# The second pass of the attention scores over 64 rows of the array, two heads side by side in two PSUM banks

## The chip, the cores and the metric

The kernel runs on one core of a Trainium2 chip. The metric is the device time of one execution in microseconds (us), as the median of several executions. The profile that is read below is that of one further execution of the same program.

## What is computed

A two-layer backbone over 512 latent tokens and 256 context tokens, 1024 wide. Each layer projects its input into three head groups (a short convolution, windowed attention with a sink, a gated linear attention over chunks), joins them in an output projection, and adds a gated feed-forward part. The change touches the attention scores alone, of which the reference says:

```python
ATT_HEADS, ATT_KV_HEADS, HEAD_DIM, BLOCK, WINDOW = 8, 2, 64, 128, 128
# latent queries, one block of 128 at a time, against the context keys and three blocks of latent keys
s_ctx = jnp.einsum('bqhgd,bkhd->bhgqk', qi, k_ctx).astype(jnp.float32)
s_loc = jnp.einsum('bqhgd,bkhd->bhgqk', qi, ks).astype(jnp.float32)
s_loc = jnp.where(valid, s_loc, -jnp.inf)
p = softmax_with_sink(jnp.concatenate([s_ctx, s_loc], axis=-1) * scale, sink).astype(v.dtype)
# context queries (first layer only) against the context keys
s = jnp.einsum('bqhgd,bkhd->bhgqk', qg, k).astype(jnp.float32) * HEAD_DIM ** -0.5
```

## The kernel before

**Products in parts.** TensorE multiplies in fp32r, which keeps fewer bits than fp32. So an operand is split into a high part (rounded to fp32r) and a low part (what is left, as fp32r), and a product is the sum of several passes. The dense products of the projections and of the feed-forward part take three passes (`dense_pass`: high by high, high by low, low by high) and write the PSUM tiles named `main`; everything else writes tiles named `bank`, of which there are five.

**The scores.** A head has 64 channels, half of the 128 rows of the array. The kernel uses the other half for the second part of the queries: in the tile `Q` of one query group, the 64 rows that are head `kv`'s own (0 to 63 for `kv` 0, 64 to 127 for `kv` 1) hold the high part of the queries and the other 64 rows the low part. `Kp[0]` holds the high part of the keys in both halves, `Kp[1]` the low part in both halves. The first pass, `Q` by `Kp[0]` over 128 rows, is high by high plus low by high in one matmul; the second, `Q` by `Kp[1]` over 128 rows, adds high by low plus low by low.

**One task of attention** (`attn_task`) is one block of 128 queries of one query group, both heads `kv`. A block of latent queries (four of them, in both layers, times four groups: 32 tasks) has 256 context keys, whose scores stand for both heads in the bank `pc` (256 columns each), and 256 (first and last block) or 384 (the two between) latent keys, whose scores stand in one bank for each head, `pl[0]` and `pl[1]`. Masks of the window are added by matmuls too (`identb` by `trib`, bf16, 128 columns, one for each outer block of a head). A block of context queries (two, in the first layer alone, times four: 8 tasks) has the 256 context keys alone. After the scores VectorE takes the maxima (`mx`, `mx2`), ScalarE the exponentials, and the probabilities are scaled, transposed by TensorE and multiplied with the values.

**What sets the order.** The dense passes are the main stream. A planner (class `Plan`) keeps an estimated clock of each engine, and after each step of the dense stream (`poll`) lets those tasks go on whose input should be there; up to three attention tasks are open at once. The estimate for a matmul (`mm`) goes by its columns, and for outputs of 128 partitions it does not depend on the rows that are contracted. The instructions that are recorded so are then ordered once more for each engine by the framework's scheduler, which may pull instructions of another stream between two of a task. Each engine then works through its queue in that order.

Beside the attention tasks run the tasks of the gated linear attention (`gla_task`), whose matmuls `gram` contract 64 rows into 64 partitions (64x64 quarters of the array), the products that write 64 partitions (128x64 halves), and those of the conditioning, which write 32 (128x32 quarters).

Of the kernel before, what the change touches and what calls it, by code (L numbers as in the profile page):

```python
# [13 lines left out]
AF = mybir.ActivationFunctionType  # L14
ALU = mybir.AluOpType
AX = mybir.AxisListType

P = 128
D = 1024
NK = D // P  # L20
SX = 512
# [298 lines left out]
def hybrid_kernel(ctx: ExitStack, tc: tile.TileContext, x, c, cx, c_ctx, w_mod, b_mod, norm1_g, norm2_g,  # L320
# [3 lines left out]
    S = Plan(tc)  # L324
# [10 lines left out]
    def bank(kind="bank"):  # L335
        return S.took(kind, psum[kind].tile([P, 512], F32, tag=kind, name=kind))

    def act_t(dt=F32):
        return S.took("act", act.tile([P, 2, T], dt, tag="act", name="act"))

    def tmp(rows=P, dt=F32):
        return S.took("t3", t3.tile([rows, T], dt, tag="t3", name="t3"))

    def sm(n, name, bufs=None):
        return small.tile([P, n], F32, tag=name, name=name, bufs=bufs)
# [281 lines left out]
    def late_consts():  # L627
        S.room(t3=1)
        lvf = tmp()
        S.pin("sp", nc.sync.dma_start(lvf, table[:, C_TL:C_COS]))  # L630
        S.pin("sp", nc.sync.dma_start(csn, table[:, C_COS:].rearrange("p (a t) -> p a t", a=2)))
        lvm = const.tile([P, 6, 64], U8, name="lvm")
        nc.gpsimd.tensor_copy(lvm.rearrange("p a b -> p (a b)"), lvf[:, C_LV - C_TL:C_BD - C_TL])
        bd = const.tile([P, P], F32, name="bd")
        nc.gpsimd.tensor_copy(bd, lvf[:, C_BD - C_TL:])
        identb = const.tile([P, P], BF16, name="identb")
        nc.gpsimd.tensor_copy(identb, ident)
        trib = const.tile([P, 2, P], BF16, name="trib")
        nc.gpsimd.tensor_copy(trib.rearrange("p a b -> p (a b)"), lvf[:, :2 * P])
        S.red(quad, ident.rearrange("p (q r) -> p r q", q=4), ALU.add)  # L640
        nc.gpsimd.tensor_scalar(nsink, psink, -1.0, None, ALU.mult)
        S.gave(lvf)
        S.room(bank=1)
        pv = bank()
        S.tr(pv[:, :V_N], vrow[:V_N, 0, :], ident[:V_N, :V_N])
        S.gave(vrow_)
        S.copy(vec[:, 16:], pv[:, 16:V_N])
        S.gave(pv)
        return lvm, bd, identb, trib
# [601 lines left out]
    def split2(full, h, sl):  # L1251
        S.acopy(h[:, 0, sl], full)
        S.tt(h[:, 1, sl], full, h[:, 0, sl].bitcast(F32), ALU.subtract)
# [210 lines left out]
    def attn_task(l, b, g, st):  # L1464

        loc = [t for t in (b - 1, b, b + 1) if 0 <= t < 4] if b < 4 else []
        tiles = [4, 5] + loc
        nl = len(loc) * P
        nkeys = 256 + nl
        yield dict(bank=3 if loc else 2, t3=2, act=lambda: int(st["ca"][g] is None))  # L1470
        if st["ca"][g] is None:
            st["ca"][g] = act_t(F32R)
        Q, Kp, Vt = st["q"][g], st["K"], st["V"]()
        pc = bank()
        pl = [bank(), bank()] if loc else [bank()]
        mx = sm(2, "mx")

        def scores(dst, kv, k0, n, stop=True):
            q_ = Q[:, kv, b * P:(b + 1) * P]
            S.mm(dst, q_, Kp[0][:, kv, k0:k0 + n], True, False)  # L1480
            S.mm(dst, q_, Kp[1][:, kv, k0:k0 + n], False, stop)
        for kv in range(2):
            scores(pc[:, kv * 256:(kv + 1) * 256], kv, SX, 256)
        S.red(mx, pc.rearrange("p (a b) -> p a b", a=2), ALU.max)
        if loc:
            mx2 = sm(2, "mx2")
            for kv in range(2):
                lm = [(i, 0 if t == b - 1 else 1) for i, t in enumerate(loc) if t != b]
                scores(pl[kv][:, :nl], kv, loc[0] * P, nl, False)
                for i, side in lm:  # L1490
                    S.mm(pl[kv][:, i * P:(i + 1) * P], identb, trib[:, side, :], False, i == lm[-1][0])
                S.red(mx2[:, kv:kv + 1], pl[kv][:, :nl], ALU.max)
            S.tt(mx, mx, mx2, ALU.max)
        sk = slice(l * 8 + g, l * 8 + g + 5, 4)
        nm = sm(2, "nm")
        S.stt(nm, mx, -0.125, nsink[:, sk], ALU.mult, ALU.min)
        den = sm(2, "den")
        den2 = sm(2, "den2")
        st["todo"][g] -= 1
        if st["todo"][g] == 0:  # L1500
            S.gave(Q)
            S.kept["attn"]["act"] = min(4, S.kept["attn"]["act"] + 1)
            if not any(st["todo"]):
                S.gave(*Kp)
        pr = [tmp(), tmp()]
        for kv in range(2):
            S.act(pr[kv][:, :256], pc[:, kv * 256:(kv + 1) * 256], AF.Exp, bias=nm[:, kv:kv + 1], scale=0.125,
                  accum_out=den[:, kv:kv + 1])
            if loc:
                S.act(pr[kv][:, 256:nkeys], pl[kv][:, :nl], AF.Exp, bias=nm[:, kv:kv + 1], scale=0.125,  # L1510
                      accum_out=den2[:, kv:kv + 1])
        S.gave(pc, *pl)
        es = sm(2, "es")
        S.tt(es, nm, psink[:, sk], ALU.add)
        S.act(es, es, AF.Exp)
        S.tt(es, es, den, ALU.add)
        if loc:
            S.tt(es, es, den2, ALU.add)
        S.recip(es, es)
        for kv in range(2):  # L1520
            S.ts(pr[kv][:, :nkeys], pr[kv][:, :nkeys], es[:, kv:kv + 1], None, ALU.mult)

        n = len(tiles)
        m = min(n, 4)
        yield dict(bank=3 if loc else 1)
        pt = [bank() for _ in range(3 if loc else 1)]
        for kv in range(2):
            for i in range(m):
                j = kv * m + i
                S.tr(pt[j // 4][:, j % 4 * P:(j % 4 + 1) * P], pr[kv][:, i * P:(i + 1) * P], ident)  # L1530
        for kv in range(2):
            if n > m:
                S.tr(pt[2][:, kv * P:(kv + 1) * P], pr[kv][:, m * P:n * P], ident)
        if loc:
            S.acopy(pr[0][:, :512], pt[0])
            S.copy(pr[1][:, :512], pt[1])
            if n > m:
                S.acopy(pr[0][:, 512:640], pt[2][:, :P])
                S.copy(pr[1][:, 512:640], pt[2][:, P:2 * P])
            S.gave(*pt[:2])  # L1540
        else:
            S.acopy(pr[0][:, :256], pt[0][:, :256])
            S.copy(pr[1][:, :256], pt[0][:, 256:])
        yield {}
        po_ = pt[-1]
        po = po_[:, 256:384]
        for i, t in enumerate(tiles):
            for kv in range(2):
                S.mm(po[kv * 64:(kv + 1) * 64], Vt[:, t, kv * 64:(kv + 1) * 64],
                     pr[kv][:, i * P:(i + 1) * P], i == 0, i == len(tiles) - 1)  # L1550
        split2(po, st["ca"][g], slice(b * P, (b + 1) * P))
        S.gave(po_, *pr)
        st["left"] -= 1
        if st["left"] == 0:
            S.gave(st["V"].t)
# [159 lines left out]
    for l in range(DEPTH):  # L1715
# [4 lines left out]
        n = SX if last else T  # L1720
# [99 lines left out]
        def after(name):  # L1820
# [21 lines left out]
            elif name == "v":  # L1842
                tasks["v"] = S.spawn(tokens_task(tmps.pop(name), st["V"]), prio=-1)
            elif name[0] == "q":
                qr = tmps.pop(name)
                rope(qr)
                S.room(act=1)
                Q = act_t(F32R)
                for kv in range(2):
                    own = slice(kv * 64, kv * 64 + 64)  # L1850
                    oth = slice(64 - kv * 64, 128 - kv * 64)
                    S.acopy(Q[own, kv, :n], qr[own, :n])
                    S.tt(Q[oth, kv, :n], qr[own, :n], Q[own, kv, :n].bitcast(F32), ALU.subtract)
                st["q"][i] = Q
                S.gave(qr)
                at_ = max(S.last, st["tk"])

                def when():
                    return max(at_, tasks["v"]["ready"]) if tasks["v"]["done"] else None
                for b in range(nblk):  # L1860
                    tasks["attn"].append(S.spawn(attn_task(l, b, i, st), prio=10 + i, group=("attn", 3), when=when))
# [10 lines left out]
        for j, name in enumerate(IN_ORDER):  # L1872
            if name in FIRST:
                if j == 0:
# [8 lines left out]
                    if l == 0:  # L1883
                        lvm, bd, identb, trib = late_consts()
# [183 lines left out]
```

## Time and profile before

| | |
|---|---|
| median of three executions | 1621.19 us (1620.47 to 1623.0) |
| the profiled execution | 1616.48 us, of which the span of the core's instructions is 1614.4 us |
| granted TensorE clock, mean | 0.998 |
| matmuls in the trace (PE) | 11562 |

The page of a profile gives, for each engine, the time in which at least one of its instructions ran, then the span in 40 slices, the DMA queues, the chain of work that ended last, and the costliest groups of instructions. A timeline lists instructions in order of time, equal neighbours merged. PE is TensorE's matmuls, PEld its weight loads, which run beside the matmuls. Ends of matmuls are modelled, and one overlaps the next; so it is the distance from one start to the next that tells what a matmul costs, not the duration in its row. In the groups, `128*64` behind a matmul is the part of the array that it uses, rows by columns, and `128x256` the operand that streams through.

### The profile page before, as it was taken

To read this page: it belongs to the slowest core of one execution; us is meant where nothing else is said; L and a number is where in the kernel's file an instruction comes from. 1 tells how busy PE (TensorE), PEld (TensorE's weight loads), DVE (VectorE), ACT (ScalarE), POOL (GpSimd) and SP (SyncE) were. 2 spreads that over 40 slices of the span, in tenths; PEclk is the share of its full clock that TensorE was granted. 3 is DMA by queue.
4 is the path that set the end of the run, shared out by engine and by line. 5 is a ranking of instruction groups with operands and counts; after the bars stand their busy time and mean duration, and the time that the engine had idled before them with its cause. 6 is when DMAs were issued, how large, how long until landed. Compare 5 with 4: busy or idle time off the path is not lost.

```text
span 1614.4 us, 29190 instructions
## 1 busy us (share of the span) xinstructions
PE 1574.5 (98%) x11562; PEld 1390.8 (86%) x11562; DVE 1220.2 (76%) x2426; ACT 755.2 (47%) x1588; POOL 103.3 (6%) x118
## 2 busy tenths in 40 slices
PE   7999999999999999999999999998999999999998
PEld 6878677888898899998999988786879999989898
DVE  5687877668886788688888776879787966757576
ACT  4445544453653243242433445464474744636354
POOL 2000000000000000000000000000001112213012
PEclk9999999999999999999999999999999999999999
DMA  9831312154224544435334342211124466848652
GB/s 267 253 96 26 93 53 79 55 169 124 60 79 147 154 141 138 141 123 151 95 109 130 94 123 66 54 38 42 66 76 122 89 148 150 173 121 160 150 123 92
DMA packets 277449, 184.32 MB, mean 114 GB/s; under 512 B 30788, under 2 KB 258624, under 8 KB 277312
## 3 DMA queue, kind: packets, MB, share of 16 engines
q1 hardware_dynamic: 251008, 155.93, 33.7%
q0 software_dynamic: 24480, 21.21, 7.7%
q10 hardware_dynamic: 1824, 5.31, 0.8%
q8 instruction: 91, 1.49, 0.4%
q14 instruction: 46, 0.38, 0.1%
HBM read 175.08 MB, written 7.34 MB: 113 GB/s over the span
## 4 chain that ended last, share of the span: by engine, by line
PE 72%; DVE 11%; DMA 5%; ACT 3%; issue 2%; DVEq 0%; SPq 0%; ACTq 0%
PE main L139 45%; PE bank L139 23%; DMA raw<-in_w_mod_dram 3%; DVE act L188 3%; PE bank L143 3%; DVE wlo L188 1%; DVE t L188 1%; DMA raw<-in_w_up_dram 1%; ACT t L155 1%; DVE t L199 1%; DVE t L216 1%; DVE act L199 1%; DVE mx L207 1%; ACT t L177 1%; ACT act L155 1%
## 5 line engine op out<-in xcount | busy, mean ns | idle before, releaser
L139 PE MATMUL main<-act,whi 128*128 128x512 f32 (+2 forms) x2772 | 667.3, 345 | 5.3 <-DVE act L199 2.5
L139 PEld LDWEIGHTS main<-act,whi 128*128 128x128 f32 x2772 | 460.4, 189 | 62.8 <-issue 12.0
L139 PE MATMUL main<-act,wlo 128*128 128x512 f32 (+2 forms) x1866 | 477.6, 333 | 2.3 <-DVE wlo L188 2.2
L139 PEld LDWEIGHTS main<-act,wlo 128*128 128x128 f32 x1866 | 314.8, 189 | 31.1 <-DVE wlo L188 4.2
L177 ACT CAST whi<-raw 128x512 fp32r<-128x512 f32 (+4 forms) x242 | 181.5, 751 | 292.4 <-PE main L139 200.9
L139 PE MATMUL bank<-act,whi 128*128 128x256 f32 (+4 forms) x1140 | 213.2, 309 | 1.7 <-DVE whi L188 1.0
L139 PEld LDWEIGHTS bank<-act,whi 128*128 128x128 f32 (+1 forms) x1140 | 177.5, 188 | 10.0 <-DVE whi L188 1.6
L139 PE MATMUL bank<-act,wlo 128*128 128x256 f32 (+4 forms) x930 | 182.0, 309 | 0.6 <-DVE wlo L188 0.6
L199 DVE SCALAR_TENSOR_TENSOR act<-main,mods,act 128x256 f32<-128x256 f32 (+1 forms) x162 | 99.3, 616 | 75.7 <-PE main L139 74.0
L139 PEld LDWEIGHTS bank<-act,wlo 128*128 128x128 f32 (+1 forms) x930 | 147.6, 189 | 5.5 <-DVE wlo L188 1.4
L188 DVE TENSOR_TENSOR wlo<-raw,whi 128x1024 fp32r<-128x1024 f32 (+4 forms) x122 | 122.7, 1006 | 22.3 <-ACT whi L177 21.5
L188 DVE TENSOR_TENSOR wlo<-raw,wlo 128x512 fp32r<-128x512 f32 x120 | 81.7, 687 | 39.5 <-ACT wlo L177 38.8
L199 DVE SCALAR_TENSOR_TENSOR t<-raw,cst,t 128x512 f32<-128x512 f32 x126 | 92.3, 747 | 21.3 <-DMA raw<-in_w_mod_dram 20.6
L188 DVE TENSOR_TENSOR whi<-raw,whi 128x512 fp32r<-128x512 f32 x120 | 81.4, 687 | 25.2 <-ACT whi L177 24.0
L155 ACT ACTIVATE t<-bank,nm 128x256 f32<-128x256 f32 (+1 forms) x144 | 69.8, 497 | 60.6 <-DVE nm L199 55.9
L177 ACT CAST wlo<-raw 128x512 fp32r<-128x512 f32 x120 | 74.6, 622 | 42.6 <-PE main L139 17.5
L177 ACT COPY t<-bank 128x512 f32<-128x512 f32 (+3 forms) x131 | 57.3, 452 | 71.8 <-PE bank L139 43.2
L139 PE MATMUL main<-act 128*128 128x256 f32 (+1 forms) x516 | 79.5, 308 | 0.0
L188 DVE TENSOR_TENSOR act<-t,act 128x512 fp32r<-128x512 f32 (+7 forms) x110 | 73.2, 682 | 7.0 <-ACT act L177 5.2
L155 ACT ACTIVATE t<-t 128x256 f32<-128x256 f32 (+3 forms) x108 | 58.1, 538 | 43.2 <-DVE t L188 42.5
L139 PE MATMUL main<-t,whi 128*128 128x512 f32 (+1 forms) x302 | 75.9, 338 | 0.0
L139 PEld LDWEIGHTS main<-act 128*128 128x128 f32 x516 | 70.9, 191 | 5.2 <-ACT t L155 0.4
(161 smaller groups left out, 2005.3 us busy)
## 6 DMA issues: line engine op xcount, KB each, us to landing
raw<-in_w_mod_dram SPq DMA_DIRECT2D x92, 512.0 KB, 4.2
raw<-in_w_up_dram SPq DMA_DIRECT2D x80, 512.0 KB, 4.0
raw<-in_w_in_dram SPq DMA_DIRECT2D x26, 512.0 KB, 3.9
t<-in_w_up_dram POOLq DMA_DIRECT2D x40, 256.0 KB, 5.5
raw<-in_w_down_dram SPq DMA_DIRECT2D x24, 384.0 KB, 4.0
raw<-in_w_down_dram SPq DMA_DIRECT2D x32, 256.0 KB, 2.9
raw<-in_w_down_dram SPq DMA_DIRECT2D x16, 320.0 KB, 3.4
raw<-in_w_up_dram POOLq DMA_DIRECT2D x20, 256.0 KB, 4.7
```

Of the source, the lines that this page charges most:

```text
L139: self.pin("pe", self.nc.tensor.matmul(out, lhsT, rhs, start=start, stop=stop, **kw))
L143: self.pin("pe", self.nc.tensor.transpose(out, in_, ident))
L155: ins = self.pin("act", self.nc.scalar.activation(out, in_, func, **kw))
L177: self.pin("act", self.nc.scalar.copy(out, in_))
L188: self.pin(eng, self._v(eng).tensor_tensor(out, a, b, op))
L199: self.pin(eng, self._v(eng).scalar_tensor_tensor(out, a, s, b, op0, op1))
L207: self.pin("dve", self.nc.vector.tensor_reduce(out, in_, AX.X, op))
L216: self.pin("dve", self.nc.vector.copy_predicated(out, mask, data))
```

## The change

The second pass of a head's scores contracts the 64 rows of its own that hold the queries' high part; the product of low by low is left out there. Head 0 uses rows 0 to 63, head 1 rows 64 to 127, and the two write different banks.

This holds for the latent keys of all 32 latent blocks, and for the 8 context blocks, for which the second head's scores move from `pc` into the bank that stood in `pl` already (it was only used later before). The context keys of the latent blocks keep their second pass over 128 rows, since there both heads stand in one bank.

The order of recording changes too: for the latent keys first both heads' first pass, then both second passes, then both heads' masks, then both maxima (before: first pass, second pass, masks and maximum of head 0, then those of head 1). The context blocks take their maxima by two reductions of 256 columns in place of one over 512.

```diff
-        def scores(dst, kv, k0, n, stop=True):
-            q_ = Q[:, kv, b * P:(b + 1) * P]
-            S.mm(dst, q_, Kp[0][:, kv, k0:k0 + n], True, False)
-            S.mm(dst, q_, Kp[1][:, kv, k0:k0 + n], False, stop)
+        cs = [pc[:, :256], pc[:, 256:] if loc else pl[0][:, :256]]
+
+        def first(dst, kv, k0, n):
+
+            S.mm(dst, Q[:, kv, b * P:(b + 1) * P], Kp[0][:, kv, k0:k0 + n], True, True)
+
+        def second(dst, kv, k0, n, stop=True):
+
+            own = slice(kv * 64, kv * 64 + 64)
+            S.mm(dst, Q[own, kv, b * P:(b + 1) * P], Kp[1][own, kv, k0:k0 + n], False, stop, more=True)
         for kv in range(2):
-            scores(pc[:, kv * 256:(kv + 1) * 256], kv, SX, 256)
-        S.red(mx, pc.rearrange("p (a b) -> p a b", a=2), ALU.max)
+            first(cs[kv], kv, SX, 256)
+            if loc:
+
+                S.mm(cs[kv], Q[:, kv, b * P:(b + 1) * P], Kp[1][:, kv, SX:], False, True, more=True)
         if loc:
+            S.red(mx, pc.rearrange("p (a b) -> p a b", a=2), ALU.max)
             mx2 = sm(2, "mx2")
+            lm = [(i, 0 if t == b - 1 else 1) for i, t in enumerate(loc) if t != b]
+            k0 = loc[0] * P
             for kv in range(2):
-                lm = [(i, 0 if t == b - 1 else 1) for i, t in enumerate(loc) if t != b]
-                scores(pl[kv][:, :nl], kv, loc[0] * P, nl, False)
+                first(pl[kv][:, :nl], kv, k0, nl)
+            for kv in range(2):
+                second(pl[kv][:, :nl], kv, k0, nl, False)
+            for kv in range(2):
                 for i, side in lm:
-                    S.mm(pl[kv][:, i * P:(i + 1) * P], identb, trib[:, side, :], False, i == lm[-1][0])
+                    S.mm(pl[kv][:, i * P:(i + 1) * P], identb, trib[:, side, :], False, i == lm[-1][0], more=True)
+            for kv in range(2):
                 S.red(mx2[:, kv:kv + 1], pl[kv][:, :nl], ALU.max)
             S.tt(mx, mx, mx2, ALU.max)
+        else:
+            for kv in range(2):
+                second(cs[kv], kv, SX, 256)
+            for kv in range(2):
+                S.red(mx[:, kv:kv + 1], cs[kv], ALU.max)
...
-            S.act(pr[kv][:, :256], pc[:, kv * 256:(kv + 1) * 256], AF.Exp, bias=nm[:, kv:kv + 1], scale=0.125,
+            S.act(pr[kv][:, :256], cs[kv], AF.Exp, bias=nm[:, kv:kv + 1], scale=0.125,
```

**What this makes of TensorE's order.** PE has 10168 matmuls in its queue before and after. Up to the first attention task of the first layer, from that layer's last to the second layer's first, and behind the second layer's last, its order is the same, matmul for matmul, and so is SyncE's queue of loads throughout. In the two stretches between, which lie at 112 to 399 us and 1023 to 1229 us of the profile, the order differs, at three places as follows. The rows give the line, the operation, output and inputs by name and the size of the output; the rows that a matmul contracts are not shown. Of two neighbouring `bank<-act` matmuls of one head the first is the first pass and the second the second pass, which now has 64 rows (but for the four on the context keys of a latent block).

The first place is on PE in the first layer, the first block of latent queries, with 256 latent keys; `bank<-act` are scores, `identb` the masks. Before:

```order
L139 MATMUL bank<-act 128x256 x6
L139 LDWEIGHTS identb
L139 MATMUL bank<-trib,identb 128x128
L139 MATMUL bank<-act 128x256 x2
L139 LDWEIGHTS identb
L139 MATMUL bank<-trib,identb 128x128
L139 MATMUL main<-act,whi 128x256 x2
```

and after:

```order
L139 MATMUL bank<-act 128x256 x8
L139 LDWEIGHTS identb
L139 MATMUL bank<-trib,identb 128x128
L139 LDWEIGHTS identb
L139 MATMUL bank<-trib,identb 128x128
L139 MATMUL main<-act,whi 128x256 x2
```

The first four of the eight are the context keys as before; then come both first passes, both second passes as neighbours, and both masks.

The second place is on PE in the first layer too, a block of context queries (`t_1227` is an operand of a `gram`). Before:

```order
L139 MATMUL bank<-act 128x256 x2
L139 MATMUL bank<-act,t_1227 64x64 x9
L139 MATMUL bank<-act 128x256 x2
L139 MATMUL bank<-act,t_1227 64x64 x15
L139 MATMUL main<-act,whi 128x256
```

and after:

```order
L139 MATMUL bank<-act 128x256 x2
L139 MATMUL main<-act,whi 128x256
L139 MATMUL main<-act,wlo 128x256
L139 MATMUL main<-act,whi 128x256 x2
L139 MATMUL main<-act,wlo 128x256
L139 MATMUL main<-act,whi 128x256
L139 MATMUL bank<-act 128x256 x2
L139 MATMUL bank<-act,t_1227 64x64 x24
```

The first two are head 0 with its two passes, the later two head 1. Here the two second passes do not stand side by side: six dense matmuls have come between the heads, and the `gram` is in one piece.

The third place is on PE in the second layer, the last group's third block, with 384 latent keys. Before, from the masks of head 0 on:

```order
L139 LDWEIGHTS identb
L139 MATMUL bank<-trib,identb 128x128
L139 LDWEIGHTS identb
L139 MATMUL bank<-trib,identb 128x128
L139 MATMUL bank<-act 128x384 x2
L139 LDWEIGHTS identb
L139 MATMUL bank<-trib,identb 128x128
L139 LDWEIGHTS identb
L139 MATMUL bank<-trib,identb 128x128
L139 MATMUL main<-act,whi 128x512
```

and after:

```order
L139 LDWEIGHTS identb
L139 MATMUL bank<-trib,identb 128x128
L139 LDWEIGHTS identb
L139 MATMUL bank<-trib,identb 128x128
L139 MATMUL main<-act,whi 128x512 x2
L139 MATMUL main<-act,wlo 128x512
L139 MATMUL main<-act,whi 128x512 x2
L139 MATMUL main<-act,wlo 128x512
L139 MATMUL bank<-act 128x384 x2
L139 LDWEIGHTS identb
L139 MATMUL bank<-trib,identb 128x128
L139 LDWEIGHTS identb
```

Head 0 and head 1 are again apart, with each head's 64-row matmul between its first pass and its masks.

Over the whole program the 80 second passes of 64 rows stand in 58 places: 22 times two heads as neighbours (11 times with 256 keys, 11 times with 384), 36 times one alone. Behind 44 of these 58 stands a mask, behind 11 another matmul of 128 rows with fp32r weights, behind 3 a `gram`. The masks stand in 64 runs before and in 44 after, the matmuls of `gram` in 34 runs before and in 32 after.

## The prediction

> **What bounds the kernel now.** I begin with the page: the busy times, then the chain of work that ended last.
>
> ```profile
> span 1614.4 us, 29190 instructions
> PE 1574.5 (98%) x11562; PEld 1390.8 (86%) x11562; DVE 1220.2 (76%) x2426; ACT 755.2 (47%) x1588; POOL 103.3 (6%) x118
> PE 72%; DVE 11%; DMA 5%; ACT 3%; issue 2%; DVEq 0%; SPq 0%; ACTq 0%
> ```
>
> TensorE is busy almost throughout, and 72% of the chain is PE. The order of PE changes only in two stretches, so the question is what limits those. The windows view of them (length, then busy time of each engine):
>
> ```profile
> 112.00:399.00 287.00, 280.02 (x2572) 227.36 (x2571) 218.46 (x522) 137.22 (x361) 6.82 (x8) 1.00 0.28 83
> 1023.00:1230.00 207.00, 199.98 (x1730) 160.57 (x1729) 170.06 (x400) 112.60 (x282) 6.06 (x8) 0.99 0.22 65
> ```
>
> PE lacks 7 us of 287 and 7 us of 207. VectorE is at 76% and 82%. Nothing but PE is near its limit: what a matmul takes there more or less moves the end, apart from these 14 us in which PE waits.
>
> The next question is the price of a matmul, which is the distance between starts. The timeline of PE, once for dense passes of 512 and 256 columns and once for a latent block with 384 keys (start, duration):
>
> ```profile
> 745.14 0.62 PE L139 MATMUL main<-act,whi 128*128 128x512 f32 x2
> 745.60 0.40 PE L139 MATMUL main<-act,wlo 128*128 128x512 f32 x1
> ...
> 747.43 0.40 PE L139 MATMUL main<-act,whi 128*128 128x256 f32 x2
> 747.67 0.28 PE L139 MATMUL main<-act,wlo 128*128 128x256 f32 x1
> ```
>
> ```profile
> 130.57 0.51 PE L139 MATMUL bank<-act 128*128 128x384 f32 x2
> 130.92 0.28 PE L139 MATMUL bank<-trib,identb 128*128 128x128 bf16 x2
> 131.03 0.62 PE L139 MATMUL bank<-act 128*128 128x384 f32 x2
> 131.49 0.28 PE L139 MATMUL bank<-trib,identb 128*128 128x128 bf16 x2
> ```
>
> Two of 512 columns take 0.46 us, two of 256 take 0.24, two of 384 take 0.35: 0.23, **0.12** and **0.175 us** each. Where the masks of head 0 stand ahead, the two matmuls of 384 take 0.46 us, 0.11 more: the weight load behind a short mask is not covered. A run of one mask, in a block with 256 keys:
>
> ```profile
> 125.79 0.23 PE L139 MATMUL bank<-trib,identb 128*128 128x128 bf16 x1
> 125.83 0.48 PE L139 MATMUL bank<-act 128*128 128x256 f32 x2
> 126.15 0.23 PE L139 MATMUL bank<-trib,identb 128*128 128x128 bf16 x1
> ```
>
> There the two behind it take 0.32 us, 0.08 more, and the mask itself 0.04 us, 0.02 less than half of 256 columns. Two masks take 0.11 us, 0.01 less than 256 columns. So a run of masks costs 0.10 or 0.06 us above its columns, as it has two masks or one; I take **0.08 us**.
>
> Now what it costs TensorE to go over to another part of the array and back. In the whole trace one matmul uses 64 rows by 128 columns, a transpose of 62 rows at 68 us; beside it I read a `gram`:
>
> ```profile
> 67.99 0.38 PE L139 MATMUL bank<-zero 128*128 128x512 bf16 x1
> 68.30 0.27 PE L143 MATMUL bank<-tab,t 62*128 62x62 f32 x1
> 68.50 0.74 PE L139 MATMUL main<-act,whi 128*128 128x512 f32 x2
> 69.08 0.40 PE L139 MATMUL main<-act,wlo 128*128 128x512 f32 x1
> ```
>
> ```profile
> 127.22 0.28 PE L139 MATMUL main<-act,wlo 128*128 128x256 f32 x1
> 127.43 0.93 PE L139 MATMUL bank<-act,t 64*64 64x64 f32 x48
> 128.29 0.50 PE L139 MATMUL main<-act,whi 128*128 128x256 f32 x2
> 128.63 0.28 PE L139 MATMUL main<-act,wlo 128*128 128x256 f32 x1
> ```
>
> From 67.99 to 69.08 are 1.09 us, in which three matmuls of 512 columns would take 3 x 0.23 = 0.69. So this visit costs 0.40 us; I take 0.04 off for the transpose itself and keep **0.36 us**. It has three parts: the visitor starts 0.31 us behind a matmul of 0.23 (0.08 lost), the next starts 0.20 us later, and then the first of the two is 0.12 us late again, since its weights are loaded only now. The `gram` shows the same on the way in: it starts 0.21 us behind a matmul of 0.12. The weight loads say what differs where a mask comes next:
>
> ```profile
> L139 PEld LDWEIGHTS bank<-act 128*128 128x128 f32 x288 | 41.3, 189 | 9.1 <-issue 4.1 <-DVE act L188 0.9 <-DVE mx L188 0.6
> L139 PEld LDWEIGHTS <-identb 128*128 128x128 bf16 x96 | 6.7, 97 | 6.4 <-issue 4.9
> ```
>
> 97 ns against 189: a visit that ends at a mask costs 0.09 us less, **0.27 us**.
>
> **The change part by part.** The rows of 64-row matmuls stand in the order of the changed kernel in 58 places.
>
> *Visits, added.* 44 end at a mask: 44 x 0.27 = 11.9 us. 11 end at fp32r weights: 11 x 0.36 = 4.0. 3 go straight on into a `gram`, which would be entered anyway; I charge the way in with its load, 0.2 each: 0.6. Sum **16.5 us**.
>
> *Passes, removed.* A matmul of 64 rows streams as many columns as one of 128. Time goes only where the two heads stand side by side and run together. That fourfold neighbours do is seen in the `gram` above: 48 matmuls in 0.86 us, 18 ns each with the way out. Of 40 tasks 22 have them so: 11 x 0.12 + 11 x 0.175 = **3.2 us** saved. In the other 18 tasks (36 lone matmuls) nothing is saved. Whether two tiles of 64x128 run together no row shows; the ends are 0 and 3.2 us, and I take 3.2, by the row of the `gram`, the nearest.
>
> *Masks, moved.* 64 runs become 44: 20 x 0.08 = **1.6 us** saved. *The `gram`, moved.* 34 runs become 32: 2 x 0.36 = **0.7 us** saved.
>
> *VectorE.* Eight reductions over 512 columns become sixteen over 256, and the maximum of head 0 comes after both heads' matmuls.
>
> ```profile
> L207 DVE TENSOR_REDUCE mx<-bank x104: 405/552/693, 113.6 to 1218.8; 128x2 f32<-128x512 f32 x40, 128x1 f32<-128x256 f32 x32, 128x1 f32<-128x384 f32 x32
> ```
>
> Two at 0.405 for one at 0.693 make 0.12 us, 1 us in all, on an engine with 24% of its time free; and head 0's reduction, 0.55 us, no longer runs beside head 1's matmuls. Dense passes stand between a task's scores and its transposes, so I cost this at nothing; without that cover, 32 tasks x 0.55 us, 18 us, would be the most. SyncE's queue keeps its order, so the loads neither gain nor lose.
>
> On PE the sum is 16.5 - 3.2 - 1.6 - 0.7 = **+11.0 us**. 34 of the 58 places lie in the first stretch, some 6 us of the sum, 24 in the second, some 5. How much of it reaches the end? The chain within the two stretches, by line:
>
> ```profile
> by line: PE main L139 43.9%; PE bank L139 26.5%; PE bank L143 7.7%; DVE act L188 7.0%; DVE t L216 2.6%; ACT t L155 2.5%; DVE t L188 1.6%; ACT t L177 1.4%; DVE wlo L188 1.2%; DVE mx L207 1.2%; issue 1.1%; ACT act L177 0.9%; DVE t L193 0.9%;
> by line: PE main L139 32.7%; PE bank L139 24.5%; DVE act L188 10.6%; PE bank L143 6.8%; DVE t L188 3.5%; DVE mx L207 3.4%; ACT t L177 2.6%; DVE t L216 2.6%; DVE wlo L188 2.3%; issue 2.2%; ACT t L155 2.2%; DVE t L193 2.0%; DVE t L203 1.1%; D
> ```
>
> PE has 78% of it in the first stretch (43.9 + 26.5 + 7.7) and 64% in the second. If the rest hid its share fully, 6 x 0.78 + 5 x 0.64 = 8 us would be left; since PE idles only 14 us of 494, I go nearer to the full sum and take **+10 us**. Against the profiled execution (1616.5 us, 1614.4 of them the span) that is 1626.5; the median shown is 1621.2, 4.7 higher, and moved by the same it is **1631 us**.
>
> **A rule weighed.** The row at 68 us does not decide alone: that transpose might have waited for the matmul ahead of it, and not for the array. The Trainium skill, page "TensorEngine Tiling (Array Packing)", section "Tiling Modes", says that a change of the mode of tiling drains TensorE, and that tiles of one mode work independently of each other. It speaks against this change. By it the visits cost what they cost above, and the sum stays at +11.0; were there no drain, the sum would be -5.5. The trace agrees for the `gram` (0.21 us behind a matmul of 0.12) and has for row halves the one row at 68 us.
>
> **The rivals.**
>
> *Row halves need no changeover (faster).* Between the first pass over 128 rows and the second over 64 nothing would drain, since all 128 columns stay in use. For it speaks a product of 96 rows:
>
> ```profile
> 81.07 0.39 PE L139 MATMUL main<-act,whi 128*128 128x512 f32 x1
> 81.30 0.40 PE L139 MATMUL main<-act,wlo 128*128 128x512 f32 x1
> 81.53 0.52 PE L139 MATMUL bank<-t,gw 96*128 96x512 f32 x2
> 81.89 0.62 PE L139 MATMUL main<-act,whi 128*128 128x512 f32 x2
> ```
>
> From 81.53 to 81.89 a matmul of 512 columns and one of 256 take 0.36 us, as they would over 128 rows (0.23 + 0.12). Against it stand the 0.08 and 0.12 us at 68 us, where 62 rows are a half. Visits at 0, the rest stays: -3.2 - 1.6 - 0.7 = -5.5 us, **1616 us**. It decides from a price per visit below 5.5 / 58 = 0.09 us.
>
> *The waits swallow it (no change).* PE idles 14 us in the two stretches for VectorE and ScalarE; if PE comes later to these places, what it waited for is there. All 11 us could go so: **1621 us**. Against it: the tasks' chains pass through PE again and again, so they come later too.
>
> *The pairs do not run together (slower still).* If head 1's 64-row matmul waits for head 0's, the 3.2 us are not saved, and its weight load, 0.1 us as at 68 us, adds 22 x 0.1 = 2.2: +16.4 us on PE, some 15 at the end, **1636 us**.
>
> That the change does not do what it says is in the forecast already: 36 of the 80 matmuls stand alone.
>
> **How the numbers follow.** Forecast, 1627 to 1634: 0.70. No changeover, 1613 to 1618: 0.10. Swallowed: 0.10. No pairs, 1634 to 1641: 0.10. About 0.2%, 3.2 us, is what a measurement of this kernel can tell from no change. Faster 0.10, same 0.10, slower 0.80. The order of some 490 us is new in detail, which may give or take 4 us whatever the matmuls cost; I widen both sides by it. From the case of no change on the one side to that of no pairs on the other: **1618 to 1641**, which leaves out the changeover-free case and little else.
>
> **What would show it.** In the timeline after, a 64-row matmul with 256 columns starts 0.21 us behind a first pass of 0.12 (right), or 0.12 behind it (no changeover). The neighbour starts within 0.02 us of it and the mask follows some 0.3 us after both (right), or 0.2 to 0.3 us lie between the two heads (no pairs). The first stretch grows by some 6 us and the second by some 4, and the others keep their lengths; if it is swallowed, PE's idle time there falls by as much. Wrong it would be if VectorE's later maxima held up the transposes: then waits of PE on `nm` would grow.

## The result, and the profile after

The changed kernel takes **1633.86 us** (median of six executions, 1631.36 to 1636.75) where the kernel before took 1622.1 in the same comparison: ratio **1.0075**, 95% interval 1.0058 to 1.0093, or 12.2 us more. The forecast was 1631 us, +10. Both the sign and the size hold, but that the size holds is in good part luck: two steps of the sum are wrong, a wait that it left out came in elsewhere, and the errors cancel.

The page of the changed kernel (span, busy times, shares of the chain), in answer to the three lines before:

```profile
span 1634.5 us, 29197 instructions
PE 1591.5 (97%) x11562; PEld 1395.7 (85%) x11562; DVE 1223.9 (75%) x2434; ACT 756.7 (46%) x1588; POOL 103.9 (6%) x118
PE 75%; DVE 9%; DMA 4%; ACT 3%; issue 2%; DVEq 0%; SPq 0%; ACTq 0%
```

The number of matmuls is the same, PE is busy 17 us longer, and the chain has more of PE (75% for 72%) and less of VectorE. The profiled execution, 1636.75 us, is the highest of the six.

Next the windows view of the two stretches whose order differs. To compare kernels, each stretch is cut here at the same two matmuls everywhere: its first scores, and the first of the dense passes that follow it in unchanged order. Columns: length, busy time of PE, PEld, DVE, ACT and POOL with the count of instructions, granted TensorE clock, DMA share, GB/s. The kernel before, by this cut:

```profile
111.90:398.50 286.60, 279.62 (x2571) 226.94 (x2570) 218.19 (x520) 136.72 (x360) 6.82 (x8) 1.00 0.28 83
1023.10:1229.30 206.20, 199.18 (x1723) 159.77 (x1722) 169.48 (x399) 112.00 (x281) 6.06 (x8) 0.99 0.22 65
```

The changed kernel:

```profile
112.10:402.20 290.10, 285.22 (x2571) 226.41 (x2571) 220.43 (x530) 137.74 (x361) 6.97 (x8) 1.00 0.27 82
1027.10:1243.10 216.00, 206.34 (x1722) 161.43 (x1722) 171.73 (x400) 114.14 (x283) 6.31 (x8) 0.98 0.21 62
```

The first stretch is **3.5 us** longer, the second **9.8**. The forecast had some 6 and some 4. It is the second stretch, with 24 of the 58 places, that grew most. PE idles 7.0 us there before (206.20 - 199.18) and 9.7 after, and the granted clock is 0.98 for 0.99. The waits of PE in the second stretch of the changed kernel say more (who waits for what: us in total, times, longest):

```profile
PE bank L139 <- ACT t L177: 4.2, 2, 3.6
PE main L139 <- ACT act L177: 3.5, 1, 3.5
```

Two waits of some 3.5 us for ScalarE stand there; before, the longest wait of PE in this stretch was 1.7 us. So something besides the price of matmuls took part.

The two stretches make 13.3 us of the 20.1 us by which the two profiled spans differ. Most of the rest lies behind the second stretch, where the order of TensorE is the same as before. The windows from the end of the second stretch to the end of the span, before and after:

```profile
1229.30:1614.40 385.10, 376.82 (x2707) 353.83 (x2705) 266.27 (x517) 194.10 (x392) 77.12 (x68) 1.00 0.59 131
1243.10:1634.50 391.40, 379.58 (x2707) 356.50 (x2705) 265.67 (x517) 192.69 (x390) 77.27 (x68) 0.99 0.58 128
```

These 6.3 us go with one wait in the changed kernel, which the kernel before does not have: TensorE waits for VectorE to prepare a weight of the feed-forward part, and VectorE waits for its load. The timeline of PE and that of VectorE there:

```profile
1403.83 0.40 PE L139 MATMUL bank<-act,whi 128*128 128x256 f32 x2
1408.16 1.22 PE L139 MATMUL bank<-act,whi 128*128 128x256 f32 x4 [3.93 <-DVE whi L188]
...
1406.81 0.69 DVE L188 TENSOR_TENSOR raw<-raw 128x512 f32<-128x512 f32 x1 [5.24 <-DMA raw<-in_w_up_dram]
```

The forecast had nothing for this part. In the profile of the second measurement of the changed kernel (below) the two stretches are 290.1 and 215.0 us, and the part behind them 388.7. In six profiles with the new order in the second layer that part took 386.3 to 391.4 us, in four with the old order there 385.1 to 386.5 (the two with matmuls added there are left out). What makes the load come late was not taken apart.

The experiments had to take apart two things that the change does at once: it gives TensorE a new order, and it makes 80 matmuls 64 rows high.

### The profile page after: what moved, and what is told of

Same layout as the page of the kernel before. It is cut to its first block, busy times and chain, and to the rows that moved or that the text cites. A ratio compares the mean times of both kernels' runs of the same rounds, so it can differ in the third digit from the quotient of the medians.

```text
span 1634.5 us, 29197 instructions
## 1 busy us (share of the span) xinstructions
PE 1591.5 (97%) x11562; PEld 1395.7 (85%) x11562; DVE 1223.9 (75%) x2434; ACT 756.7 (46%) x1588; POOL 103.9 (6%) x118
## 4 chain that ended last, share of the span: by engine, by line
PE 75%; DVE 9%; DMA 4%; ACT 3%; issue 2%; DVEq 0%; SPq 0%; ACTq 0%
PE main L139 48%; PE bank L139 24%; PE bank L143 3%; DVE act L188 2%; DMA raw<-in_w_mod_dram 2%; DMA raw<-in_w_up_dram 2%; DVE t L188 1%; DVE wlo L188 1%; ACT t L155 1%; DVE t L199 1%; DVE t L216 1%; DVE act L199 1%; DVE whi L188 1%; ACT act L177 1%; ACT whi L177 0%
## 5 line engine op out<-in xcount | busy, mean ns | idle before, releaser
L207 DVE TENSOR_REDUCE mx<-bank 128x1 f32<-128x256 f32 (+2 forms) x112 | 57.4, 532 | 27.9 <-PE bank L139 27.1
```

The lines of the kernel that those rows point to most:

```text
L207: self.pin("dve", self.nc.vector.tensor_reduce(out, in_, AX.X, op))
```

## The experiments

The ratios are against runs of the kernel before on the same chip, with 95% intervals. Of single profiles, a stretch that nobody touched varied by 1.5 to 2 us from one kernel to the next (286.6 and 288.1 us in the first stretch, 204.5 to 206.2 in the second).

### The new order with 128 rows, and the old order with 64

**New order, 128 rows.** The change as it is, but the second pass contracts 128 rows again. The order of every engine is that of the changed kernel, row for row.

```diff
-            own = slice(kv * 64, kv * 64 + 64)
-            S.mm(dst, Q[own, kv, b * P:(b + 1) * P], Kp[1][own, kv, k0:k0 + n], False, stop, more=True)
+            S.mm(dst, Q[:, kv, b * P:(b + 1) * P], Kp[1][:, kv, k0:k0 + n], False, stop, more=True)
```

> The changed kernel with its second pass over 128 rows again (low by low is back in); order, banks and maxima as after the change, row for row on every engine. If the changeover of the array is the cost, all 58 visits go and with them the 22 pairs: against the kernel before, only the masks (20 runs fewer x 0.08 us) and the gram (2 x 0.36) remain, -2.3 us, ratio 0.9986 (0.996 to 1.001). If the new order and the later maxima are the cost, it stays as slow as the change: +8 us or more, ratio 1.005 or above.

Measured: 1623.22 us, ratio **1.0039** (1.0020 to 1.0057). Slower than before, by 6 us, although it has fewer runs of masks and of `gram` and none of the 58 visits. That lies between the two expectations (0.9986, and 1.005 or above), and its interval reaches the second alone. Its windows:

```profile
113.50:398.00 284.50, 277.48 (x2570) 226.30 (x2570) 219.45 (x530) 137.21 (x361) 6.98 (x8) 1.00 0.28 84
1020.00:1234.10 214.10, 202.89 (x1724) 162.55 (x1723) 171.52 (x400) 113.82 (x283) 6.30 (x8) 0.97 0.21 63
```

The first stretch does what the theory said (2.1 us shorter than before; two more kernels below have this order there, and both come out within 0.1 us of this one). The second is **7.9 us longer**: most of what the change costs there, it costs with 128 rows too.

Since this kernel and the changed one run the same order, they also give the price of a 64-row visit directly. Timeline of PE (start, duration), a block with 256 and one with 384 latent keys, in the kernel with 128 rows:

```profile
126.94 1.22 PE L139 MATMUL bank<-act 128*128 128x256 f32 x8
128.00 0.29 PE L139 MATMUL bank<-trib,identb 128*128 128x128 bf16 x2
...
132.53 0.51 PE L139 MATMUL bank<-act 128*128 128x384 f32 x2
132.89 0.29 PE L139 MATMUL bank<-trib,identb 128*128 128x128 bf16 x2
132.99 0.62 PE L139 MATMUL bank<-act 128*128 128x384 f32 x2
133.45 0.29 PE L139 MATMUL bank<-trib,identb 128*128 128x128 bf16 x2
```

and in the changed kernel (a merged row carries the part of the array of its first matmul; the rows with `64*128` are from narrower windows, which show the 64-row matmuls by themselves):

```profile
125.88 1.29 PE L139 MATMUL bank<-act 128*128 128x256 f32 x8
126.78 0.38 PE L139 MATMUL bank<-act 64*128 64x256 f32 x2
127.10 0.29 PE L139 MATMUL bank<-trib,identb 128*128 128x128 bf16 x2
...
131.47 0.70 PE L139 MATMUL bank<-act 128*128 128x384 f32 x2
131.73 0.44 PE L139 MATMUL bank<-act 64*128 64x384 f32 x1
132.11 0.29 PE L139 MATMUL bank<-trib,identb 128*128 128x128 bf16 x2
132.20 0.79 PE L139 MATMUL bank<-act 128*128 128x384 f32 x2
132.92 0.28 PE L139 MATMUL bank<-trib,identb 128*128 128x128 bf16 x2
```

From the scores to their masks, a lone second pass makes 0.64 us out of 0.36 and 0.72 out of 0.46: a visit costs **0.28 and 0.26 us**, where the forecast had 0.27. The pair makes 1.22 out of 1.06, +0.16: one visit of 0.27 less one saved matmul of 0.12. So the two heads' 64-row matmuls do run together; had the second waited for the first, the pair would have cost more than a lone one. The rows with `64*128` show the sign that the prediction named: the last first pass starts at 126.57, the two 64-row matmuls 0.21 us behind it and within 0.01 us of each other, and their mask 0.32 us after them.

**Old order, 64 rows.** The kernel before, with the second pass on the latent keys over 64 rows, each alone behind its first pass, 62 of them ahead of a mask: 64 visits and no pair.

```diff
+            own = slice(0, P) if k0 == SX else slice(kv * 64, kv * 64 + 64)
-            S.mm(dst, q_, Kp[1][:, kv, k0:k0 + n], False, stop)
+            S.mm(dst, q_[own], Kp[1][own, kv, k0:k0 + n], False, stop)
```

> The kernel before, in its own order row for row, with the second pass of the latent keys over 64 rows (low by low left out there; the context blocks as before): 64 lone visits, no pair. By the changeover's price 62 x 0.27 + 0.36 + 0.2 = 17.3 us on TensorE, some 15.5 at the end, ratio 1.0095 (1.007 to 1.012). If row halves need no changeover, nothing changes: 0.999 to 1.002.

Measured: 1629.28 us, ratio **1.0074** (1.0062 to 1.0086), near the lower end of what the theory had (1.007 to 1.012) and far from no change. The windows:

```profile
113.00:407.60 294.60, 288.36 (x2571) 228.78 (x2570) 219.77 (x520) 136.79 (x360) 6.81 (x8) 1.00 0.26 80
1029.10:1241.60 212.50, 207.26 (x1723) 161.79 (x1723) 170.12 (x399) 112.32 (x281) 6.07 (x8) 0.99 0.21 63
```

PE is busy 8.7 and 8.1 us longer than before, 16.8 together, and 64 x 0.27 is 17.3. The stretches grew by 8.0 and 6.3: PE waits 0.7 and 1.8 us less, so some of the price goes into waits that stood there. The old order has no wait of 3.5 us in the second stretch, and without one the stretch is 3.5 us shorter than in the changed kernel, although it has more visits there (32 for 24).

### All heads as neighbours

In every task the second passes are ordered behind both first passes, so all 40 pairs stand side by side; low by low is left out as in the change.

```diff
-                second(pl[kv][:, :nl], kv, k0, nl, False)
+                S.behind(second(pl[kv][:, :nl], kv, k0, nl, False), fi)
...
-                second(cs[kv], kv, SX, 256)
+                S.behind(second(cs[kv], kv, SX, 256), fi)
```

> The changed kernel, in which each task's two 64-row matmuls are held back until both first passes are issued, so that all 40 stand side by side: 40 visits in place of 58, 40 pairs in place of 22, 32 runs of masks. By the changeover's price: visits 32 x 0.27 + 5 x 0.36 + 3 x 0.2 = 11.0 us, pairs save 24 x 0.12 + 16 x 0.175 = 5.7, masks 32 x 0.08 = 2.6, gram 0.7: +2.0 us against the kernel before, ratio 1.001 (0.999 to 1.004). If the order is the cost, it is as slow as the change, 1.005 to 1.009.

Measured: 1626.93 us, ratio **1.0057** (1.0045 to 1.0069). The changed kernel, run again beside it:

> The change once more, on the same chip as the three others: ratio 1.0075 as measured, 1.006 to 1.009.

1631.03 us, ratio 1.0090 (1.0075 to 1.0105). More pairs and fewer visits help, by some 4 us where the prices gave 9, but the result is still slower than before, in the range that was expected if the order is the cost (1.005 to 1.009). The windows of the kernel with 40 pairs:

```profile
113.40:399.90 286.50, 280.89 (x2571) 223.94 (x2571) 219.61 (x530) 137.55 (x361) 6.76 (x8) 1.00 0.27 83
1023.90:1240.70 216.80, 206.23 (x1724) 161.37 (x1723) 171.79 (x400) 113.71 (x283) 6.45 (x8) 0.96 0.21 62
```

The gain is in the first stretch alone (286.5 for 290.1), where it is back at the time of before. The second is as long as in the changed kernel (216.8): its length does not follow the number of visits, though its clock, 0.96 for 0.98, hides part of what fewer visits gain.

### One layer at a time

The changed code stands in one layer, the code of before in the other: the change in the first layer alone, in the second alone, and the new order with 128 rows in the first alone. The order in each layer is that of the kernel the code comes from.

```diff
+        if l == 0:
             cs = [pc[:, :256], pc[:, 256:] if loc else pl[0][:, :256]]
...
+        else:
+            cs = [pc[:, :256], pc[:, 256:]]
...
```

> The change in the first layer alone; the second layer as before. Orders of the first layer as after the change, of the second as before. Theory now: the changeover costs some 5.5 us in the first stretch, the order gives back 2.1 there, and the other 9.5 us of the change come from the second stretch, most of them from one place in its new order: +3.4 us, ratio 1.002 (1.001 to 1.0035). Rival, every changeover costs the end its 0.25 us wherever it stands (34 of 58 in the first layer): more than half of the change, +7 us or more, 1.0045 or above.

> The change in the second layer alone; the first layer as before. Theory: +9.5 us, ratio 1.006 (1.0045 to 1.0075), of which 8 from the order. Rival, by the count of changeovers (24 of 58): +5 us, 1.003.

> In the first layer the order of the change, but the second pass over 128 rows (low by low in); the second layer as before. Theory: the fewer runs of masks and of gram remain, -2.1 us in the first stretch, ratio 0.9987 (0.9975 to 1.000). Rival, the new order or the later maxima cost as such in either layer: slower than before, 1.001 or above.

Measured:

| | us | ratio | 95% interval |
|---|---|---|---|
| change in the first layer | 1624.49 | 1.0038 | 1.0023 to 1.0053 |
| change in the second layer | 1631.83 | 1.0076 | 1.0063 to 1.0089 |
| new order, 128 rows, first layer | 1617.57 | 0.9994 | 0.9982 to 1.0006 |

The windows of the third, first layer and second:

```profile
112.90:397.50 284.60, 277.58 (x2571) 226.32 (x2571) 219.53 (x530) 137.22 (x361) 6.94 (x8) 1.00 0.28 84
1023.00:1227.50 204.50, 197.60 (x1724) 158.74 (x1723) 169.49 (x399) 111.83 (x281) 6.07 (x8) 1.00 0.22 66
```

In the first layer the new order costs nothing, and its stretch is 2 us shorter; in the second, the layer with fewer visits, the change costs twice as much as in the first. The third line, the fastest of all, cannot be told from before; new order and 128 rows in both layers took 1.0039, so in the times the order of the second layer costs some 0.45%, 7 us. The first line is 0.2% above its expectation (1.002), and its interval holds the rival's bound too (1.0045), so it does not decide between them; its profiled execution was the second shortest of twelve, which spread from 1619 to 1631.6 us, so little hangs on it. The first two lines add up to 1.14%, more than the 0.75% to 0.90% of the whole change, and why is open.

### What TensorE waits for in the second layer

Of the two long waits, one stands in the output projection, whose passes on the last head group need the gate of that group. The timeline of PE with the new order and 128 rows (in brackets how long the engine was idle, and for whom):

```profile
1188.43 0.40 PE L139 MATMUL main<-act,wlo 128*128 128x512 f32 x1
1192.67 0.80 PE L139 MATMUL main<-act,whi 128*128 128x512 f32 x1 [3.84 <-ACT act L177]
1193.39 1.98 PE L139 MATMUL bank<-t,t 128*64 128x128 f32 x16
1195.30 1.97 PE L143 MATMUL bank<-tab,t 128*128 128x128 f32 x8
```

and that of ScalarE (left out are an attention task's exponentials):

```profile
1186.23 0.62 ACT L177 CAST act<-t 128x512 fp32r<-128x512 f32 x1
...
1188.79 1.28 ACT L155 ACT_TABLE_LOAD   x1
1190.09 0.60 ACT L155 ACTIVATE t<-main 128x512 f32<-128x512 f32 x1
1190.70 1.28 ACT L166 ACT_TABLE_LOAD   x1
1192.00 0.62 ACT L177 CAST act<-t 128x512 fp32r<-128x512 f32 x1
```

A gate is a Silu (`t<-main`) between two loads of ScalarE's tables and a cast. The casts of two gates start 5.8 us apart (1186.23 and 1192.00), with an attention task's exponentials in between, and TensorE has nothing else to do: the projection's passes for one gate are done at 1188.8 and the next gate is not there. In the kernel before:

```profile
1179.98 0.62 ACT L177 CAST act<-t 128x512 fp32r<-128x512 f32 x1
...
1190.78 0.62 ACT L177 CAST act<-t 128x512 fp32r<-128x512 f32 x1
```

10.8 us lie between the two, TensorE has dense passes and other tasks' products left for all of it, and no wait of PE falls there. The number of table loads in the whole program is the same (15); it is where the tasks fall in the order that differs.

Behind the wait the granted clock is low: over 10 us the mean is 0.68, in the kernel with the new order and 128 rows:

```profile
1188.00:1198.00 10.00, 6.16 (x31) 4.32 (x29) 4.96 (x10) 6.84 (x13) 0.00 (x0) 0.68 0.09 27
```

**The wait filled.** To separate the wait from the clock behind it, 16 matmuls of zeros of 512 columns were put into the open sum of the output projection at that place; they change no value.

```diff
+                    for _ in range(fill if k == n - 1 else 0):
+                        nc.tensor.matmul(pt, zero[:, :P], zero, start=False, stop=False)
```

> The kernel with 128 rows in the order of the change (e1_rows128), and in the second layer 16 matmuls of zeros (0.22 us each, 3.5 us) added into the output projection's sum at the place where TensorE waits 3.8 us for the gate of the last head group; they change no value. If the loss there is also the halved clock behind the wait (6.8 us at half, so 3.4 us), the fill keeps the clock up: 3 us faster than e1_rows128, ratio to the kernel before 1.002 (1.0005 to 1.003), no half clock near 1190 us. If it is the wait alone, no gain, 1.004, and if the zeros come on top, 1.006.

Measured: 1625.2 us, ratio 1.0033 (1.0020 to 1.0046), against 1.0039 (1.0020 to 1.0057) without the filling: in the times the difference is within the uncertainty, and the 3 us that were expected do not show (1.002). The profile shows what the filling does at its place. Timeline of PE (the record of one of the 16 is missing):

```profile
1188.55 3.40 PE L751 MATMUL main<-zero 128*128 128x512 bf16 x15
...
1193.44 1.09 PE L139 MATMUL bank<-t,t 128*64 128x128 f32 x16
1194.47 1.09 PE L143 MATMUL bank<-tab,t 128*128 128x128 f32 x8
```

and the windows of the same 10 us and of the whole stretch:

```profile
1188.00:1198.00 10.00, 9.56 (x68) 5.87 (x68) 6.20 (x12) 6.96 (x13) 0.00 (x0) 1.00 0.08 24
1020.00:1231.80 211.80, 203.95 (x1737) 161.98 (x1738) 171.50 (x400) 113.72 (x283) 6.31 (x8) 0.98 0.22 63
```

The clock is at 1.00, and the two groups of 16 and 8 matmuls take 1.09 us each where they took 1.98 and 1.97. With useless work in place of the wait the stretch is 2.3 us shorter (211.8 for 214.1 us), little more than single profiles vary. So at this place the wait costs twice: its own length, and a slow clock for some microseconds after it. The end does not gain it in this profile: behind the stretch TensorE waits 4.2 us for a weight of the feed-forward part where it waited 1.4, and that part is 390.5 us for 386.3.

That the clock takes part in the cost of the order is not a matter of one profile. Over all their executions the mean granted clock is 0.9935 with the new order and 128 rows, 0.996 for the kernel before in the same comparison, and 0.997 with the old order and 64 rows. By an estimate, 0.0025 of 1617 us is 4 us of the 6.

### The price of a visit where nothing waits

140 matmuls of zeros (bf16, 256 columns) in the feed-forward products of the second layer, in open sums and without effect on a value, once over 64 rows and once over 128, at the same places.

```diff
+                if kk == 2 and self.l == 1:
+                    nc.tensor.matmul(pt, zero[:64, :P], zero[:64, :w], start=False, stop=False, skip_group_check=True)
```

> The kernel before, with 140 matmuls of zeros added inside the second layer's feed-forward products (256 columns, 64 rows, bf16, into the open sum, no value changes), where TensorE hardly waits. Theory (a changeover costs 0.09 us in and 0.10 us out, and 0.10 us more for the fp32r weights that are then loaded uncovered): 140 x (0.12 + 0.28) = +56 us, ratio 1.035 (1.030 to 1.040). Rival (a changeover costs only what reached the end in this study, about 8.3 us for 58, 0.14 us): 140 x (0.12 + 0.14) = +36 us, ratio 1.022. Neither mechanism (no changeover): as with 128 rows, 1.0105.

> The same 140 matmuls of zeros at the same places over 128 rows: no changeover is left. Theory and rival: 140 x 0.12 us = +17 us, ratio 1.0105 (1.008 to 1.013); the distance to the kernel with 64 rows is the price of 140 visits.

Measured: 1672.46 us with 64 rows (ratio 1.0297, 1.0255 to 1.0338), 1631.48 with 128 (1.0056, 1.0035 to 1.0076). Both ratios lie some 0.5% below what was expected; the kernel before ran at 1621.97 in this comparison, which was made on another chip, and at 1617 to 1619 in the other two, and why the ratios are low is open. The distance between the two kernels does not depend on it: 41.0 us for 140 visits, **0.29 us** each, where the theory had 0.28 net and the rival 0.14 (36 - 17 us, by 140). Timeline of PE, 64 rows:

```profile
1420.46 0.28 PE L1171 MATMUL main<-zero 64*128 64x256 bf16 x1
...
1421.48 0.88 PE L139 MATMUL bank<-act,whi 128*128 128x256 f32 x6
```

and 128 rows:

```profile
1278.50 0.28 PE L1171 MATMUL main<-zero 128*128 128x256 bf16 x1
...
1279.33 0.87 PE L139 MATMUL bank<-act,whi 128*128 128x256 f32 x6
```

From the zeros to the second group are 1.02 us with 64 rows and 0.83 with 128, so 0.19 of the price lies behind the visitor; the other 0.09 is its own late start (in the median it starts 0.21 us behind the matmul ahead of it with 64 rows, and 0.12 with 128). Here, where TensorE hardly waits, the whole price reaches the end.

## Why the prediction came out right, and where it was wrong

**Visits and passes: right.** The changed kernel less the kernel with its order and 128 rows gives them alone. PE is busy 7.7 us longer in the first stretch (285.22 - 277.48) and 3.4 in the second, where the clock is 0.98 for 0.97, some 2 us of 214 that hide part of the difference. Together, with the clock's part estimated, some 13 us; the forecast had 16.5 - 3.2 = 13.3. The pairs run together, and the two rivals *Row halves need no changeover* and *The pairs do not run together* fall with it. The Trainium skill, page "TensorEngine Tiling (Array Packing)", section "Tiling Modes", says that a change of mode drains TensorE; the trace agrees for row halves in that a visit costs time, 0.27 us where it ends at a mask. That this time is a drain, no row shows.

**Masks and `gram`: right in the first layer.** -2.1 us of PE there, of -2.3 forecast for both layers. In the second, PE is busy 3.7 us longer at a lower clock, and the saving can't be seen.

**How much reaches the end: wrong.** The step took +10 of +11, "nearer to the full sum", because PE idles only 14 us. Of some 13 us of visits less pairs 7.5 reached the end (290.10 - 284.50 and 216.00 - 214.10); PE idles 2.1 and 1.6 us less in return, and the lower clock of the kernel with 128 rows makes up the rest. In the times the difference of the two kernels is 0.36% to 0.51%, 6 to 8 us. The shares of PE in the chain, 78% and 64%, which the step worked out (8 us) and set aside, were the better guide in this order, where 7.5 of 13 is 58%; on the old order it is 12 of 17 us, 70%. In the feed-forward part all of it reached the end. So the rival *The waits swallow it* was right about 3.7 us of the 13.

**The order itself: wrong.** It stood in the forecast as "may give or take 4 us whatever the matmuls cost", and the sum took it at nothing beyond masks and `gram`. In the first layer that holds (0.9994). In the second the new order costs 7.9 us with no 64-row matmul at all: PE idles 11.2 us for 7.0, and the clock is 0.97 for 0.99, by an estimate 4 us of 214. The split therefore failed (3.5 and 9.8 us for 6 and 4), and the total was right by luck, because too much was charged for visits at the end and too little for the order: -2.1 + 5.6 in the first stretch, +7.9 + 1.9 in the second.

**The other stretches: wrong.** They were to keep their lengths. Behind the second stretch the two profiles of the changed kernel are 6.3 and 3.6 us longer than that of the kernel before, at a wait for a weight's load.

**VectorE's later maxima: right.** ScalarE's waits for `nm` before the exponentials, in the kernel before and then in the changed one (us in total, times, longest):

```profile
ACT t L155 <- DVE nm L199: 55.9, 24, 4.8
```

```profile
ACT t L155 <- DVE nm L199: 57.0, 27, 4.8
```

They are the same within some 1 us, and PE's wait for `nm` in the second stretch, 1.7 us before, is gone.

What stays open is why the order that came out for the second layer leaves TensorE nothing to do between the two gates. That was not taken apart, nor was an order with the gates held apart tried. The other long wait of that layer (3.6 us, at a `gram`) was not filled either, and the late load behind the layer's attention was not traced to its cause. No version here beats the kernel before by more than its uncertainty.

## What to carry to other kernels

Here a matmul over half the rows saved nothing unless its neighbour ran in the other half, and a visit to half the array between full-height matmuls cost more (0.27 us) than the 0.12 or 0.175 us that a pair saves. By these numbers, as an estimate, a run would need three pairs of 256 columns, or two of 384, to pay; none was run. When a change also moves the order, run the new order with the old arithmetic first: here that alone was about half of the whole effect, a gain of 2 us in one layer and a loss of 8 in the other. In the two stretches the share of the engine in the chain was a better estimate of what reaches the end than its share of busy time; the remainder depends on what the new order makes wait, also in stretches whose own order is the same.

## What the hardware showed beyond that

Waits of TensorE of 3.6 to 3.9 us were followed by a clock far below full for several microseconds: over 10 or 11 us that hold one such wait each, the mean granted clock is 0.66 and 0.68 (new order with 128 rows, at 1114 and 1188 us) and 0.69 (the changed kernel, at 1404 us). Where one was filled, 2.3 us came back on top of its 3.84 us, in one pair of profiles; by that estimate it cost about 1.6 times its length. The Trainium skill, page "TensorE: Matmul & The Clock Gate", part 1, has a window of 3.4 us of idling after which the clock is halved; the trace agrees in size, but shows more: in the kernel before, two waits of 1.7 and 1.4 us with matmuls between them were followed by a low clock too. Its window there, with PE busy 7.33 of 11 us and the clock at 0.85:

```profile
1117.00:1128.00 11.00, 7.33 (x102) 5.17 (x100) 9.75 (x26) 6.38 (x17) 0.00 (x0) 0.85 0.18 50
```
